# Contracting the value matmuls of the 16 by 16 corner over 128 rows instead of 32 in a forgetting-attention layer

## The chip, the cores and the metric

The kernel runs on one core of one Trainium2 chip. The metric is the device time of one execution in microseconds (us); lower is better. Engines are called as the profile calls them: PE is TensorE's matmuls, PEld its weight loads, DVE VectorE, ACT ScalarE, POOL GpSimd, SP the engine that issues DMAs.

## The reference

One layer over 16 learned tokens followed by 2048 tokens of width 1024. What matters here is its attention, 16 heads of width 64:

```
s = q_t . k_s * 64**-0.5 + c_t - c_s        (c: running sum of log sigmoid of a forget logit)
mask: key position <= query position
p = softmax(s);  o_t = sum_s p[t, s] v_s
```

The rest of the layer is an input norm, one input projection, a pooling mixer, gates, an output projection and an output norm. All of it is float32. The kernel gets float32 accuracy from pairs of float32r numbers (a high part and a low part, `ph` and `pl` of the exponentials).

## The kernel before, in words

The program has three stages. The first computes the projections, the row maxima of the attention and the pooling mixer. The second (phase B) does the attention, and mixes the matmuls of the output projection into it as filler (tiles `d<-wh,xm`, `d<-wl,xm`). The third finishes the output projection and the norm. Every engine but SP executes its instructions in the order in which the code emits them (`in_order`).

In phase B the work goes in 64 chunks: one for each head `h` and each block `j` of 512 queries, `j` from 0 to 3. The keys of a chunk are taken in units, written by `units(j)`: the 4j+1 full units of 128 keys by 512 queries, then a unit of 400 queries, then a last unit with three places of 272, 144 and 16 queries, since the causal mask leaves less and less of the block. The 16 learned tokens shift keys against queries, so that the last 16 queries of a block still need 16 keys of the next key tile. This is the 16 by 16 corner, the place with `w == NM`. Its keys stand in rows 112 to 127: the score matmuls take the 128 keys that end with these 16, and `mask_c` sends all rows but the last 16 to exp(-1e30) = 0. The corner's value rows are loaded into rows 112 to 127 of the tile `vc`.

For each unit `m` the loop emits `emit_s(m)` (scores into PSUM tile `s`, four buffers; two exponentials on ACT), up to four filler matmuls, `emit_pl(m)` (the low part `pl` on DVE, which frees the buffer of `s`), and `emit_pv(m - 4)`: the value matmuls, with the exponentials as the moving operand and the values as the weights. `xo` sums the products with `ph`; `yo` sums the products with `pl` and, through the weights `zo` (64 columns of zeros and two of ones), the softmax denominator. In chunks with j from 1 to 3 two more matmuls, `yo<-th,zo` and `yo<-tl,zo`, add a denominator that POOL and DVE have summed. At the end of a chunk ACT copies `yo` out (`c1`, shown as `c`), and DVE combines it with `xo`.

In the kernel before, the three value matmuls of a corner use rows 96 to 127 of weights and moving operand alone; only these rows of `vc` are set to zero (two memsets on POOL, one for each of the two sets of buffers).

Of the kernel before, what the change touches and what calls it, by code (L numbers as in the profile page):

```python
# [16 lines left out]
P = 128  # L17
NM = 16
# [5 lines left out]
DH = 64  # L24
# [11 lines left out]
def f32(ap):  # L36
    return ap.bitcast(F32)
# [3 lines left out]
def kernel(  # L41
# [20 lines left out]
    nc = tc.nc  # L62
# [35 lines left out]
    nc = NC()  # L98
    mm = nc.tensor.matmul

    def dma(out, in_):
        out, in_ = out[tuple(slice(None) for _ in out.shape)], in_[tuple(slice(None) for _ in in_.shape)]
        nc.sync.dma_start(
            out.bitcast(F32) if out.dtype == F32R else out, in_.bitcast(F32) if in_.dtype == F32R else in_
        )
# [12 lines left out]
    def dtile(name, shape, dt):  # L118
        return dram.tile(shape, dt, tag=name, name=name)

    # rows of a head: c high and low, k high, k low, q low, q high, -max high and low
    kqd = dtile("kqd", [H, 260, L], F32)
    vd = [dtile(f"vd{c}", [8, P, NKT, P], F32) for c in range(2)]
    fd = dtile("fd", [H, L], F32)
# [321 lines left out]
    off = fp.tile([P, 1], F32, tag="off", name="off")  # L446
# [279 lines left out]
    def kv_set(pl, s):  # L726
        ka = pl.tile([68, L], F32R, tag=f"ka{s}", name="ka")
        kb = pl.tile([P, L], F32R, tag=f"kb{s}", name="kb")
        vt = pl.tile([P, NKT - 1, P + 2], F32R, tag=f"vt{s}", name="vt")
        vc = pl.tile([P, 4, P + 2], F32R, tag=f"vc{s}", name="vc")  # L730
        nc.gpsimd.memset(f32(ka[0:2, :]), 1.0)
        nc.gpsimd.memset(f32(vc[96:P]), 0.0)
        for v in (vt, vc):
            nc.gpsimd.memset(f32(v[:, :, P : P + 2]), 1.0)
        kas.append(ka)
        kbs.append(kb)
        vts.append((vt, vc))

    kv_set(kvs[0], 0)
    zo = kvs[0].tile([P, DH + 2], F32R, tag="zo", name="zo")  # L740
    nc.vector.memset(f32(zo[:, 0:DH]), 0.0)
# [10 lines left out]
    def load_kv(h, i):  # L752
        ka, kb, (vt, vc) = kas[h % 2], kbs[h % 2], vts[h % 2]
        half, h8 = divmod(h, 8)
        if i == loaded[h]:
            loaded[h] += 1
            c0, c1 = 512 * i + (NM if i else 0), 512 * (i + 1) + NM
            dma(ka[2:68, c0:c1], kqd[h, 0:66, c0:c1])
            dma(kb[:, c0:c1], kqd[h, 2:130, c0:c1])
            dma(vt[:, 4 * i : 4 * i + 4, 0:P], vd[half][h8, :, 4 * i : 4 * i + 4, :])  # L760
            dma(vc[P - NM : P, i, 0:P], vd[half][h8, :NM, 4 * i + 4, :])
# [6 lines left out]
    def load_q(n):  # L768
        h, j = seqn[n]
        qa = qas[n % NQ]  # L770
        qb = kvs[0].tile([P, 512], F32R, tag="qb", name="qb", bufs=NQ)
        sl = slice(NM + 512 * j, NM + 512 * (j + 1))
        dma(qa[0:2, :], kqd[h, 258:260, sl])
        dma(qa[4:68, :], kqd[h, 194:258, sl])
        dma(qb, kqd[h, 130:258, sl])
        qt[n] = (qa, qb)
# [6 lines left out]
    fetched = [0]  # L783

    def prefetch(n, nv):
        """Loads at most one piece of keys and values ahead of head order, and queries two steps ahead."""
        k = 0
        while kvq:
            h, i = kvq[0]
            near = any(t[0] == h and t[1] >= i for t in seqn[n : n + 2])  # L790
            if h >= 2 and last_use[h - 2] >= nv or (k and not near) or first_use[h] > n + 5:
                break
            load_kv(h, i)
            kvq.popleft()
            k += 1
        while fetched[0] < min(NB, n + 3):
            load_q(fetched[0])
            fetched[0] += 1
# [12 lines left out]
    pso = pool(phase_b, "pso", space=PSUM)  # L811
    bp = pool(phase_b, "bp")
    kv_set(bp, 1)

    wsl = {}
# [60 lines left out]
    order = [t for t in (*range(4, 8), *range(4), *range(8, 12)) if t not in EARLY] + EARLY  # L876
# [36 lines left out]
    def after(d, fn):  # L913
        state["id"] = state.get("id", 0) + 1
        post.append((state["round"] + d, state["id"], fn))

    def chunk_end(p, j):
        sl = slice(512 * j, 512 * (j + 1))
        st = gt.tile([P, 8], F32, tag="st", name="st", bufs=2)
        dma(st, sd[p][:, sl].rearrange("a (b c) -> a b c", c=8))  # L920

        def s1():
            nc.vector.reciprocal(st, st)
            dma(rd[p][:, sl].rearrange("a (b c) -> a b c", c=8), st)
            rb = gt.tile([P, 512], F32, tag="rb", name="rb", bufs=2)
            for e in range(2):
                dma(rb[DH * e : DH * (e + 1), :], rd[p][e : e + 1, sl].broadcast_to([DH, 512]))
            sg = gt.tile([P, 512], F32, tag="sg", name="sg", bufs=2)
            dma(sg, gd[p][:, sl])

            def s2():
                a = araw.pop((p, j))
                for t in (rb, sg):
                    nc.gpsimd.tensor_tensor(out=a, in0=a, in1=t, op=ALU.mult)

                def s3():
                    am = gt.tile([P, 2, 512], F32R, tag="am", name="am", bufs=2)
                    nc.vector.tensor_copy(out=am[:, 0], in_=a)
                    nc.gpsimd.tensor_tensor(out=am[:, 1], in0=a, in1=f32(am[:, 0]), op=ALU.subtract)
                    dma(xmix[0][:, p, :, sl], am)  # L940
                    gated.add((p, j))

                after(2, s3)

            after(4, s2)

        after(4, s1)
# [67 lines left out]
    def emit_pv(m):  # L1015
        n, i, u, nu = seq[m]
        h, j = seqn[n]
        vt, vc = vts[h % 2]
        ph, pl, places = units_state.pop(m)
        if i == 0:  # L1020
            xy[0] = pso.tile([P, 512], F32, tag="x", name="xo", bufs=2)
            xy[1] = pso.tile([P, 512], F32, tag="y", name="yo", bufs=1)
        xo, yo = xy[0], xy[1]
        last_u = i == nu - 1
        np_ = len(places)
        full = i < 4 * j
        for idx, (kt, q0, w, off) in enumerate(places):
            first = i == 0 and idx == 0
            sl = slice(off, off + w)
            rows, v = (slice(96, P), vc[:, j]) if w == NM else (slice(0, P), vt[:, kt])  # L1030
            mm(
                xo[:, q0:512], v[rows, 0:P], ph[rows, sl],
                start=first, stop=last_u and idx == np_ - 1,
            )
            if not full:
                mm(yo[0 : DH + 2, q0:512], zo[rows], ph[rows, sl], start=first, stop=False)
        if last_u and j:
            for t in accs.pop(n):
                mm(yo[0 : DH + 2, :], zo, t, start=False, stop=False)
        for idx, (kt, q0, w, off) in enumerate(places):  # L1040
            rows, v = (slice(96, P), vc[:, j]) if w == NM else (slice(0, P), vt[:, kt])
            mm(
                yo[0 : DH + 2, q0:512], v[rows, DH:], pl[rows, off : off + w],
                start=full and i == 0 and idx == 0, stop=last_u and idx == np_ - 1,
            )
        if last_u:
            c1 = bp.tile([65, 512], F32, tag="c1", name="c1", bufs=2)
            nc.scalar.copy(out=c1, in_=yo[0:65, :])
            t = bp.tile([DH, 512], F32, tag="t", name="t", bufs=2)
            nc.vector.tensor_tensor(out=t, in0=xo[DH:P, :], in1=c1[0:DH, :], op=ALU.add)  # L1050
            p, e = divmod(h, 2)
            if e == 0:
                araw[p, j] = gt.tile([P, 512], F32, tag="araw", name="araw", bufs=6)
            sl = slice(512 * j, 512 * (j + 1))
            nc.vector.tensor_tensor(
                out=araw[p, j][DH * e : DH * (e + 1), :], in0=xo[0:DH, :], in1=t, op=ALU.add
            )
            dma(sd[p][e : e + 1, sl], c1[64:65, :])
            if e == 1:
                after(1, lambda: chunk_end(p, j))  # L1060
# [19 lines left out]
    def weight(m):  # L1080
        n, i, u, nu = seq[m] if m < nseq else seq[-1]
        return 2.0 if i < nu - 2 else 1.0

    LEAD, TAIL = 24, 24
    for m in range(nseq + LAG):
        if m < nseq:
            emit_s(m)
        if m >= LEAD:
            if m < nseq - TAIL:
                w = [weight(t) for t in range(m, nseq - TAIL)]  # L1090
# [3 lines left out]
            k = min(int(state["fill"]), 4)  # L1094
# [139 lines left out]
```

## Time and profile before

| what | value |
|---|---|
| median of 3 runs | 2431.03 us (2428.52 to 2432.9) |
| span of the profiled execution | 2432.5 us |
| PE busy | 2366.8 us, 97% of the span, 11706 matmuls |
| PEld busy | 1947.5 us, 80% |
| DVE busy | 1430.4 us, 59% |
| ACT busy | 960.6 us, 39% |
| POOL busy | 716.2 us, 29% |

The span runs from the first to the last instruction of one profiled execution. No separate device time of that execution is given; its span lies inside the range of the three timed runs, 1.5 us above their median. PE is busy almost all the time. Every row shows L86, the line of the helper that emits all instructions in order, so the rows are told apart by their tiles (`out<-in`) and shapes: `32*128 32x16` is a matmul over 32 rows with 128 columns of weights and 16 columns streamed. Matmuls overlap in the records (the next starts before the one before has ended), so what a matmul costs is read from the distance between the starts of two neighbours, not from its duration.

### The profile page before, as it was taken

To read this page: it belongs to the slowest core of one execution; us is meant where nothing else is said; L and a number is where in the kernel's file an instruction comes from. 1 tells how busy PE (TensorE), PEld (TensorE's weight loads), DVE (VectorE), ACT (ScalarE), POOL (GpSimd) and SP (SyncE) were. 2 spreads that over 40 slices of the span, in tenths; PEclk is the share of its full clock that TensorE was granted. 3 is DMA by queue.
4 is the path that set the end of the run, shared out by engine and by line. 5 is a ranking of instruction groups with operands and counts; after the bars stand their busy time and mean duration, and the time that the engine had idled before them with its cause. 6 is when DMAs were issued, how large, how long until landed. Compare 5 with 4: busy or idle time off the path is not lost.

```text
span 2432.5 us, 32725 instructions
## 1 busy us (share of the span) xinstructions
PE 2366.8 (97%) x11706; PEld 1947.5 (80%) x11706; DVE 1430.4 (59%) x2116; ACT 960.6 (39%) x1813; POOL 716.2 (29%) x531
## 2 busy tenths in 40 slices
PE   6999999999999999999999899999999999999998
PEld 5778799898898988988887677777777777776787
DVE  6631145644655556545433578778778777777356
ACT  4431221211212222111111577777777777766000
POOL 4730021222223314230101134344353544444000
PEclk9999999999999999999999999999999999999999
DMA  7853222222222212222223657566566657555955
GB/s 254 262 162 92 61 85 61 96 63 78 88 62 88 81 60 88 68 92 75 75 81 111 174 159 210 153 189 181 168 187 179 199 168 215 161 164 158 286 187 164
DMA packets 317506, 333.59 MB, mean 137 GB/s; under 512 B 27744, under 2 KB 241072, under 8 KB 317312
## 3 DMA queue, kind: packets, MB, share of 16 engines
q1 hardware_dynamic: 317344, 331.51, 44.4%
q8 instruction: 92, 1.51, 0.3%
q14 instruction: 70, 0.57, 0.1%
HBM read 207.43 MB, written 124.00 MB: 136 GB/s over the span
## 4 chain that ended last, share of the span: by engine, by line
PE 91%; DVE 3%; DMA 2%; issue 1%; ACT 1%; POOL 0%; SPq 0%; DVEq 0%; ACTq 0%; POOLq 0%
PE d L86 59%; PE s L86 12%; PE yo L86 8%; PE mx L86 6%; PE xo L86 5%; DVE pl L86 1%; PE tr L86 1%; DMA xm<-xa 1%; DMA wu<-in_wut_dram 0%; SPq L86 0%; DVE acc L86 0%; DMA xt<-in_x_dram 0%; DVE s L86 0%; DMA wv<-in_wv_dram 0%; DMA kb<-kqd 0%
## 5 line engine op out<-in xcount | busy, mean ns | idle before, releaser
L86 PE MATMUL d<-hh,wh 128*128 128x412 f32 (+2 forms) x1472 | 561.4, 381 | 0.0
L86 PE MATMUL d<-hl,wh 128*128 128x412 f32 (+2 forms) x1472 | 538.6, 366 | 0.0
L86 PE MATMUL d<-hh,wl 128*128 128x412 f32 (+2 forms) x1472 | 538.4, 366 | 0.0
L86 DVE TENSOR_REDUCE mxs<-mx 128x1 f32<-128x912 f32 (+14 forms) x416 | 358.3, 865 | 279.1 <-PE mx L86 274.5
L86 DVE TENSOR_TENSOR pl<-s,ph 128x512 fp32r<-128x512 f32 (+2 forms) x576 | 376.3, 664 | 185.8 <-ACT s L86 179.6
L86 ACT ACTIVATE ph<-s 128x512 fp32r<-128x512 f32 (+2 forms) x576 | 335.0, 582 | 186.6 <-PE s L86 171.9
L86 PE MATMUL d<-wh,xm 128*128 128x512 f32 x1024 | 355.0, 403 | 4.6 <-DMA xm<-xa 3.8
L86 ACT ACTIVATE s<-s 128x512 f32<-128x512 f32 (+2 forms) x576 | 332.4, 577 | 0.0
L86 PEld LDWEIGHTS d<-hl,wh 128*128 128x128 f32 x1472 | 278.5, 189 | 23.1
L86 PEld LDWEIGHTS d<-hh,wl 128*128 128x128 f32 x1472 | 277.1, 188 | 23.4
L86 PEld LDWEIGHTS d<-hh,wh 128*128 128x128 f32 x1472 | 280.7, 191 | 18.2
L86 PE MATMUL s<-qa,ka 68*128 68x512 f32 (+4 forms) x704 | 265.2, 377 | 15.9 <-DVE pl L86 15.9
L86 POOL TENSOR_TENSOR wl<-wst,wh 128x1024 fp32r<-128x1024 f32 x40 | 96.2, 2405 | 576.4 <-ACT wh L86 576.3
L86 PE MATMUL s<-qb,kb 128*128 128x512 f32 (+4 forms) x704 | 253.0, 360 | 0.0
L86 POOL TENSOR_TENSOR tu<-ph 128x512 f32<-128x512 f32 x144 | 190.9, 1328 | 154.4 <-ACT ph L86 128.3
L86 PE MATMUL xo<-ph,vt 128*128 128x512 f32 (+3 forms) x640 | 233.0, 368 | 0.0
L86 PEld LDWEIGHTS d<-wh,xm 128*128 128x128 f32 x1024 | 193.5, 190 | 44.4 <-issue 3.3
L86 PE MATMUL yo<-pl,vt 128*66 128x512 f32 (+3 forms) x640 | 223.7, 366 | 0.9 <-ACT c L86 0.9
L86 PE MATMUL mx<-ka,qa 66*128 66x512 f32 (+5 forms) x704 | 199.4, 350 | 6.6 <-ACT qa L86 3.8
L86 PE MATMUL d<-wl,xm 128*128 128x512 f32 x512 | 205.6, 402 | 0.0
L86 PEld LDWEIGHTS s<-qa,ka 68*128 68x128 f32 x704 | 134.8, 191 | 71.6 <-DVE pl L86 27.4
L86 PEld LDWEIGHTS mx<-ka,qa 66*128 66x128 f32 x704 | 133.0, 190 | 23.8 <-ACT qa L86 5.2
(143 smaller groups left out, 3079.0 us busy)
## 6 DMA issues: line engine op xcount, KB each, us to landing
xm<-xp SPq DMA_DIRECT2D x32, 1024.0 KB
xm<-xa SPq DMA_DIRECT2D x20, 1024.0 KB
vd<-vs SPq DMA_DIRECT2D x32, 512.0 KB
vt<-vd SPq DMA_DIRECT2D x64, 256.0 KB
qb<-kqd SPq DMA_DIRECT2D x64, 256.0 KB
xa<-am SPq DMA_DIRECT2D x32, 512.0 KB
xp<-pm SPq DMA_DIRECT2D x32, 412.0 KB
kqd<-lo SPq DMA_DIRECT2D x64, 206.0 KB
```

The source lines that it names most:

```text
L86: return in_order(f(*a, **k))
```

## The change

The three value matmuls of each corner take all 128 rows of `vc`, `zo`, `ph` and `pl` instead of rows 96 to 127, and the two memsets clear all of `vc`, so that rows 0 to 111 of it are zeros. The result is the same, since those rows multiply exponentials that are zero. No instruction is added, removed or moved on any engine: the order of the program's rows is the same on PE, DVE, ACT and SP, and on POOL two rows change their shape, from 32x520 to 128x520.

```diff
-        nc.gpsimd.memset(f32(vc[96:P]), 0.0)
+        nc.gpsimd.memset(f32(vc), 0.0)
...
-            rows, v = (slice(96, P), vc[:, j]) if w == NM else (slice(0, P), vt[:, kt])
+            v = vc[:, j] if w == NM else vt[:, kt]
             mm(
-                xo[:, q0:512], v[rows, 0:P], ph[rows, sl],
+                xo[:, q0:512], v[:, 0:P], ph[:, sl],
                 start=first, stop=last_u and idx == np_ - 1,
             )
             if not full:
-                mm(yo[0 : DH + 2, q0:512], zo[rows], ph[rows, sl], start=first, stop=False)
+                mm(yo[0 : DH + 2, q0:512], zo, ph[:, sl], start=first, stop=False)
...
-            rows, v = (slice(96, P), vc[:, j]) if w == NM else (slice(0, P), vt[:, kt])
+            v = vc[:, j] if w == NM else vt[:, kt]
             mm(
-                yo[0 : DH + 2, q0:512], v[rows, DH:], pl[rows, off : off + w],
+                yo[0 : DH + 2, q0:512], v[:, DH:], pl[:, off : off + w],
                 start=full and i == 0 and idx == 0, stop=last_u and idx == np_ - 1,
             )
```

## Rows read from the trace of the kernel before

**Rows 1.** The page, part 4: shares of the chain that ended last, by engine.

```profile
PE 91%; DVE 3%; DMA 2%; issue 1%; ACT 1%; POOL 0%; SPq 0%; DVEq 0%; ACTq 0%; POOLq 0%
```

**Rows 2.** Windows: phase B; us, busy us (instructions) of PE, PEld, DVE, ACT, POOL, clock, DMA.

```profile
1359.20:2246.30 887.10, 870.29 (x4347) 657.53 (x4345) 689.16 (x1061) 649.64 (x1242) 377.22 (x288) 0.99 0.61 180
```

**Rows 3.** Timeline of PE, end of one chunk with j = 1: start us, duration us, instruction.

```profile
1809.31 0.29 PE L86 MATMUL yo<-ph,zo 128*66 128x272 f32 x1
1809.44 0.23 PE L86 MATMUL xo<-ph,vt 128*128 128x144 f32 x1
1809.50 0.23 PE L86 MATMUL yo<-ph,zo 128*66 128x144 f32 x1
1809.66 0.27 PE L86 MATMUL xo<-ph,vc 32*128 32x16 f32 x1
1809.80 0.20 PE L86 MATMUL yo<-ph,zo 32*66 32x16 f32 x1
1809.92 0.45 PE L86 MATMUL yo<-th,zo 128*66 128x512 f32 x1
1810.21 0.39 PE L86 MATMUL yo<-tl,zo 128*66 128x512 f32 x1
1810.44 0.35 PE L86 MATMUL yo<-pl,vt 128*66 128x272 f32 x2
1810.72 0.22 PE L86 MATMUL yo<-pl,vc 32*66 32x16 f32 x1
1810.87 0.50 PE L86 MATMUL s<-qa,ka 68*128 68x512 f32 x1
1811.21 0.39 PE L86 MATMUL s<-qb,kb 128*128 128x512 f32 x1
```

**Rows 4.** Timeline of PEld at the same place.

```profile
1809.44 0.14 PEld L86 LDWEIGHTS yo<-ph,zo 128*66 128x66 f32 x1
1809.66 0.18 PEld L86 LDWEIGHTS xo<-ph,vc 32*128 32x128 f32 x1
...
1809.92 0.13 PEld L86 LDWEIGHTS yo<-th,zo 128*66 128x66 f32 x1
1809.98 0.14 PEld L86 LDWEIGHTS yo<-tl,zo 128*66 128x66 f32 x1
...
1810.72 0.13 PEld L86 LDWEIGHTS yo<-pl,vc 32*66 32x66 f32 x1
1810.87 0.19 PEld L86 LDWEIGHTS s<-qa,ka 68*128 68x128 f32 x1
1810.98 0.19 PEld L86 LDWEIGHTS s<-qb,kb 128*128 128x128 f32 x1
```

**Rows 5.** Timeline of PE, end of one chunk with j = 0, first and last.

```profile
1800.01 0.23 PE L86 MATMUL yo<-ph,zo 128*66 128x144 f32 x1
...
1801.26 0.40 PE L86 MATMUL s<-qb,kb 128*128 128x512 f32 x1
```

**Rows 6.** Groups of PE by shape: busy us, mean ns, idle us before.

```profile
L86 PE MATMUL xo<-ph,vc 32*128 32x16 f32 x64 | 17.4, 272 | 0.0
```

**Rows 7.** Timeline of PE, the scores of one corner.

```profile
1804.11 0.26 PE L86 MATMUL s<-qa,ka 68*128 68x16 f32 x1
1804.22 0.26 PE L86 MATMUL s<-qb,kb 128*128 128x16 f32 x1
```

**Rows 8.** Waits of PEld in phase B: us in total, times, longest us.

```profile
PEld s L86 <- DVE pl L86: 27.4, 27, 3.0
PEld yo L86 <- ACT c L86: 2.7, 6, 1.2
```

**Rows 9.** Waits of PEld from 1355 to 1400 us.

```profile
PEld s L86 <- DVE pl L86: 8.9, 8, 2.4
```

**Rows 10.** Windows from 1355 to 1400 us, instructions on tile `vc` alone (PE, PEld, POOL).

```profile
1355.00:1400.00 45.00, 1.48 (x6) 0.93 (x6) 0.64 (x2) 0.96 0.77 216
```

**Rows 11.** Timeline of POOL, the second of the two memsets.

```profile
1359.24 0.53 POOL L86 MEMSET vc<- 32x520 f32 x1 [27.39 <-PE d L86]
```

## The prediction

> **What bounds the kernel now.** I read the page first, for who sets the end: in the chain of work that ended last PE holds 91% [rows 1]. Then the windows, for the stage of the change: phase B takes 887.1 us, PE is busy in 870.3 of them, DVE in 689.2 (78%) and ACT in 649.6 (73%) [rows 2]. So a microsecond that PE does not need there is, to first order, a microsecond of the kernel, and the question is only what PE spends at the corners.
>
> For that I read the timeline of PE around one corner, start to start [rows 3]. Full-height matmuls are spaced by their columns: 272 columns take 0.13 us (1809.31 to 1809.44), 144 columns 0.06 (1809.44 to 1809.50), 512 columns 0.23 (1810.21 to 1810.44). The neighbours of the 32-row matmuls are not. After the 144 columns at 1809.50 the corner's `xo` matmul starts 0.16 later, the corner's `yo` 0.14 after it, `th` 0.12 after that, though 16 columns are streamed in each of the last two; `th` itself, 512 columns, holds its successor up for 0.29 instead of 0.23; the corner's `pl` matmul starts 0.28 after the pair of 272 and 144 columns, which need 0.13 + 0.06; then 0.15 and 0.34 follow.
>
> The weight loads say why [rows 4]. A load normally runs ahead of its matmul: that of the 144-column `yo` starts at 1809.44, while the matmul before it starts, 0.06 ahead of its own. At the four places where the number of rows changes (128 to 32, 32 to 128, and both again) the load starts together with its own matmul: 1809.66, 1809.92, 1810.72, 1810.87, the same starts as in [rows 3]. So at each change of height the load is not started early, and PE stands bare for it. Loads of one height follow each other quicker: 66 columns in 0.06 (1809.92 to 1809.98), 128 columns in 0.11 (1810.87 to 1810.98).
>
> **The change part by part.** It removes no instruction. It makes three matmuls and three loads per chunk 128 rows high, 64 chunks [rows 6], and with that removes all four changes of height.
>
> The kernel before has no 128-row matmul of 16 columns with these weights, so I build the new spacing from the nearest rows: each step is the longer of the columns streamed ahead and the next load.
> - 144-column `yo` to corner `xo`: the load of 128 columns, 0.11 (before: 0.16).
> - corner `xo` to corner `yo`: the load of 66 columns, 0.06 (before: 0.14).
> - corner `yo` to `th`: 0.06 (0.12); `th` to `tl`: 0.23 (0.29); `tl` to `pl`: 0.23 (0.23).
> - the `pl` pair: 0.13 + 0.06 = 0.19 (0.28).
> - corner `pl` to `s<-qa`: the load of 128 columns, 0.11 (0.15); `qa` to `qb`: 0.23 (0.34).
>
> The new sum is 0.11 + 0.06 + 0.06 + 0.23 + 0.23 + 0.19 + 0.11 + 0.23 = 1.22 us. Before, it is 1811.21 - 1809.50 = 1.71 us [rows 3]: 0.49 us less. A chunk with j = 0 lacks `th` and `tl`: 1801.26 - 1800.01 = 1.25 us before [rows 5], and 0.11 + 0.06 + 0.06 + 0.19 + 0.11 + 0.23 = 0.76 after, again 0.49 less. Over 64 chunks that is 31.4 us.
>
> The uncertain step is 0.06 for a 66-column load behind 16 columns. The other bound is the nearest 16-column neighbours of full height: the two score matmuls of a corner start 0.11 apart [rows 7], but load 128 columns of weights each. If all 16-column steps cost 0.11, the three steps at 0.06 (into corner `yo`, into `th`, into corner `pl`) rise by 0.05 each, and a chunk gains 0.34, in all 21.8 us. Below that lies no gain at all (the second rival). I take 0.06, because [rows 4] shows it on this very load (`zo`, 66 columns), and because [rows 3] has a 66-column matmul 0.06 behind 144 columns, so such a load fits into 0.06.
>
> The memset grows from 32 to 128 rows with the same 520 elements in each. It takes 0.53 us [rows 11]; I bound it between 0.53 (rows in parallel) and 2.1 (four times). POOL stood idle for 27.39 us before it, and only the loads into the second set wait for it, so it costs nothing; if that cover were gone, 1.6 us, twice.
>
> What is late next: PE reaches the next scores 0.49 us sooner after each corner, and a buffer of `s` is free only when DVE has made `pl`. Before, PEld waits for this 27 times [rows 8], in 576 units. Where it waits, a saving made just ahead turns into waiting. If each of the 27 swallowed one whole saving, 27 x 0.49 = 13.2 us would be given back. They come in bunches, though: in the first 45 us there are 8 of them [rows 9] and only 3 chunk ends (6 matmuls on `vc`, two of an end [rows 10]), so 8 waits can swallow 3 savings. By that ratio 27 waits swallow about 10 savings, 4.9 us. The other wait that can grow is that for ACT's copy of `yo`, whose only buffer the next chunk needs: 6 times, 2.7 us in all [rows 8]. The copy starts when the last `yo` ends, and so moves ahead with it; I take nothing for it. After the change DVE would be busy for 689 of about 861 us, 80%, still no bound.
>
> The sum against the profiled execution: 2432.5 - 31.4 + 4.9 = 2406.0. Its span is 1.5 us above the median of the runs; against the median that is 2404.5, and I say 2404 us, 1.1% less.
>
> **The rivals.**
>
> *The small step costs 0.11 whatever the weights.* Then 21.8 us are gained, less a third of the given-back time, since the savings are smaller by a third (3.3 us): 2431.0 - 18.5 = 2412.5. For it speaks [rows 7], the only full-height matmuls of 16 columns; against it the 0.06 between two loads [rows 4].
>
> *The change does not do what it says: the gaps belong to the narrow corner, not to its height.* The loads of 32 rows last no less than those of 128 (0.18 against 0.19 [rows 4]), so no load gets cheaper or dearer, and the three matmuls keep their place. Then the time stays at 2431. Against it speak the 0.29 of `th` and the 0.34 of `s<-qa`: they are full-height, have 512 columns, and are held up only because the matmul ahead is of another height. The Trainium skill ("TensorE: Matmul & The Clock Gate", "Why this matters for your kernels") says that one matmul over 32 rows takes the same time as one over 128, the gain lying in several at once; by that rule alone the sum would be zero and the time 2431. The same skill ("TensorEngine Tiling (Array Packing)", "Key Properties") says that a change of tiling mode drains the engine; by that rule the height costs something after all, and the late loads of [rows 4] agree with it.
>
> *Slower: a full-height load cannot start while a full-height matmul is in flight.* Then each of five loads would wait for the end of the matmul ahead: 0.23 + 0.18 into corner `xo`, 0.27 + 0.14 into corner `yo`, 0.20 + 0.14 into `th`, 0.23 + 0.14 into corner `pl` (taking the 144-column `pl` as long as the 144-column `yo`), 0.22 + 0.19 into `s<-qa`, in sum 1.94 [rows 3, 4]; with `th`, `tl` and `qa` at 0.23 each and the 0.13 of the first `pl`, 2.76 us against 1.71. That is +1.05 us for 64 chunks, +67 us, 2498. It decides from two of the five on: a serial step costs some 0.3 more than in my list (0.41 against 0.11 into corner `xo`), so two use up the gain of 0.49. Against it: the score matmuls of a corner are full-height, last 0.26 each and still start 0.11 apart [rows 7]; serial they would be 0.45 apart. The Trainium skill ("TensorE: Matmul & The Clock Gate", Part 3, "The mechanism") has such a rule: loads overlap matmuls in flight only where the row group differs; by it the time would be the 2498 above, and the 0.11 of [rows 7] does not agree.
>
> **How the numbers follow.** My forecast gets 0.76, the dearer small step 0.11, no effect 0.08, slower 0.03; 0.02 are left for a gain beyond the forecast's. The forecast's own range goes from 2431.0 - 31.4 = 2399.6 (nothing given back) to 2431.0 - 31.4 + 13.2 = 2412.8 (every wait swallows a saving). The first rival lies inside it or at its edge; with the spread of the runs (2 us either way) the range is 2397 to 2415. It leaves out the other two rivals. About 0.2% (4.9 us) is what a measurement of this kernel can tell from no change: faster 0.88, same 0.08, slower 0.04.
>
> **What the profile after would show.** The loads of corner `xo`, `th`, corner `pl` and the next scores start ahead of their matmuls again; corner `xo` starts 0.11 us behind the 144 columns, corner `yo` and `th` 0.06 apart; `th` to `tl` takes 0.23; the whole end of a chunk 1.2 us instead of 1.7. Phase B is about 27 us shorter, and the wait of the score loads for DVE grows by some 5 us. If the small steps stand at 0.11, the first rival is right; if 1.7 us remain, the second. I would be wrong most easily if DVE's waits multiplied, so that PE's gain came out as idle time: then PE's ends would be shorter and phase B not.

## The result and the profile after

| | before | after |
|---|---|---|
| median | 2430.08 us (4 runs, 2428.52 to 2432.9) | 2403.17 us (4 runs, 2401.99 to 2404.49) |
| span of the profiled execution | 2432.5 us | 2402.8 us |
| ratio of the times, 95% interval | | 0.9881 [0.9867, 0.9895] |

The kernel became 26.9 us faster; 2404 had been forecast. In a second comparison beside other kernels (label e8_changed_again below) the same change gave 2402.76 against 2430.31 us.

The chain of work that ended last, page part 4, answers to [rows 1]; PE's share has not moved, it is still the bound:

```profile
PE 91%; DVE 3%; DMA 2%; ACT 1%; issue 1%; POOL 0%; SPq 0%; DVEq 0%; ACTq 0%; POOLq 0%
```

The window of phase B, with the columns of [rows 2] and over the same instructions (4347 matmuls, 4345 loads in both): 857.4 us, where it was 887.1, and PE busy 840.2 instead of 870.3. The 30 us lie in the stage of the change and in PE's own work. The mean granted clock of TensorE is 0.992 of its full 2.4 GHz in either profiled execution, so the clock does not explain the difference.

```profile
1360.05:2217.47 857.42, 840.23 (x4347) 644.45 (x4345) 686.58 (x1061) 648.67 (x1242) 380.80 (x288) 0.99 0.63 186
```

The timeline of PE at the end of the same chunk as in [rows 3]:

```profile
1791.93 0.29 PE L86 MATMUL yo<-ph,zo 128*66 128x272 f32 x1
1792.06 0.23 PE L86 MATMUL xo<-ph,vt 128*128 128x144 f32 x1
1792.13 0.23 PE L86 MATMUL yo<-ph,zo 128*66 128x144 f32 x1
1792.19 0.22 PE L86 MATMUL xo<-ph,vc 128*128 128x16 f32 x1
1792.27 0.20 PE L86 MATMUL yo<-ph,zo 128*66 128x16 f32 x1
1792.33 0.43 PE L86 MATMUL yo<-th,zo 128*66 128x512 f32 x1
1792.60 0.39 PE L86 MATMUL yo<-tl,zo 128*66 128x512 f32 x1
1792.83 0.35 PE L86 MATMUL yo<-pl,vt 128*66 128x272 f32 x2
1793.01 0.17 PE L86 MATMUL yo<-pl,vc 128*66 128x16 f32 x1
1793.04 0.48 PE L86 MATMUL s<-qa,ka 68*128 68x512 f32 x1
1793.35 0.40 PE L86 MATMUL s<-qb,kb 128*128 128x512 f32 x1
```

The same eleven rows, in the same order. From the 144-column `yo` to the second score matmul it was 1.71 us; now it is 1793.35 - 1792.13 = 1.22. The weight loads there (PEld, as [rows 4]):

```profile
1792.13 0.19 PEld L86 LDWEIGHTS xo<-ph,vc 128*128 128x128 f32 x1
1792.24 0.14 PEld L86 LDWEIGHTS yo<-ph,zo 128*66 128x66 f32 x1
1792.30 0.14 PEld L86 LDWEIGHTS yo<-th,zo 128*66 128x66 f32 x1
...
1792.95 0.14 PEld L86 LDWEIGHTS yo<-pl,vc 128*66 128x66 f32 x1
1793.02 0.19 PEld L86 LDWEIGHTS s<-qa,ka 68*128 68x128 f32 x1
1793.12 0.19 PEld L86 LDWEIGHTS s<-qb,kb 128*128 128x128 f32 x1
```

The loads run ahead again. That of the corner's `xo` starts at 1792.13, with the matmul before it and 0.06 ahead of its own; before, it started together with its own matmul. The loads now follow each other at their own pace, 0.10 to 0.11 us after a load of 128 columns, 0.06 to 0.07 after one of 66. The load for `s<-qa` starts only 0.02 ahead of its matmul, but it follows the load before it at that pace.

The waits of PEld in phase B, as [rows 8], and the memset, as [rows 11]:

```profile
PEld s L86 <- DVE pl L86: 26.3, 26, 3.6
PEld yo L86 <- ACT c L86: 4.3, 7, 1.6
```

```profile
1360.09 0.53 POOL L86 MEMSET vc<- 128x520 f32 x1 [27.41 <-PE d L86]
```

DVE's wait has not grown, that for ACT's copy has by 1.6 us. Clearing 128 rows takes the 0.53 us of 32.

### The profile page after: what moved, and what is told of

Its sections match the earlier page's. It is cut to its first block, busy times and chain, and to the rows that moved or that the text cites. A ratio compares the mean times of both kernels' runs of the same rounds, so it can differ in the third digit from the quotient of the medians.

```text
span 2402.8 us, 32724 instructions
## 1 busy us (share of the span) xinstructions
PE 2336.9 (97%) x11706; PEld 1934.7 (81%) x11706; DVE 1427.3 (59%) x2116; ACT 959.5 (40%) x1813; POOL 719.3 (30%) x531
## 4 chain that ended last, share of the span: by engine, by line
PE 91%; DVE 3%; DMA 2%; ACT 1%; issue 1%; POOL 0%; SPq 0%; DVEq 0%; ACTq 0%; POOLq 0%
PE d L86 60%; PE s L86 12%; PE yo L86 8%; PE mx L86 6%; PE xo L86 5%; DMA xm<-xa 1%; PE tr L86 1%; DVE pl L86 1%; ACT ph L86 0%; DMA wu<-in_wut_dram 0%; DMA xt<-in_x_dram 0%; DVE s L86 0%; DMA wv<-in_wv_dram 0%; ACT s L86 0%; DVE mxs L86 0%
## 5 line engine op out<-in xcount | busy, mean ns | idle before, releaser
L86 POOL TENSOR_TENSOR wl<-wst,wh 128x1024 fp32r<-128x1024 f32 x40 | 96.2, 2404 | 576.7 <-ACT wh L86 576.6
L86 PEld LDWEIGHTS s<-qa,ka 68*128 68x128 f32 x704 | 134.9, 192 | 69.0 <-DVE pl L86 26.3
```

The costliest lines, as they stand in the source:

```text
L86: return in_order(f(*a, **k))
```

## The experiments

Two accounts were to be told apart. The height account: each *change* of the number of rows costs PE a fixed time, whichever matmuls stand there. The matmul account: each of the three 32-row matmuls is dear in itself. After the change both are gone, so its result fits either. In each experiment below I read the same stretch of PE's timeline, from the start of the 272-column `yo` to the start of the second score matmul of the same chunk: 1811.21 - 1809.31 = 1.90 us before [rows 3], 1793.35 - 1791.93 = 1.42 after. The chunk shown is a usual one: the median of this stretch over the chunks with j from 1 to 3 is 1.90 us before and 1.42 after. All times are medians; each of the two sets of four kernels shared its runs of the kernel before (2429.06 us for the first four, 2430.31 for the others).

**One of the three matmuls back on 32 rows.** In the changed kernel:

```diff
+            rows = slice(96, P) if w == NM else slice(0, P)
...
-                yo[0 : DH + 2, q0:512], v[:, DH:], pl[:, off : off + w],
+                yo[0 : DH + 2, q0:512], v[rows, DH:], pl[rows, off : off + w],
```

> The changed kernel, with the corner's pl matmul alone back on rows 96 to 127: two changes of height per chunk, one 32-row matmul. Height theory (each change of the number of rows costs a fixed price, and the four of a chunk cost 0.48 us together): in the kernel before, the steps around this matmul took 0.159 + 0.150 + 0.338 us against 0.067 + 0.028 + 0.314 after the change, 0.24 us more, so 64 x 0.24 = 15 us of the 27 come back and the time is about 2418 us. Matmul theory (each of the three 32-row matmuls is dear in itself, a third of the gain each): 9 us come back, 2412 us.

Measured 2417.17 us, ratio to before 0.9946 [0.9934, 0.9958]; the gain over the kernel before of its own set is 11.9 us, where the whole change gains 26.9 to 27.6, so some 15 us came back. The matmul account had 9. PE's timeline:

```profile
1798.18 0.29 PE L86 MATMUL yo<-ph,zo 128*66 128x272 f32 x1
...
1799.07 0.35 PE L86 MATMUL yo<-pl,vt 128*66 128x272 f32 x2
1799.35 0.22 PE L86 MATMUL yo<-pl,vc 32*66 32x16 f32 x1
1799.50 0.50 PE L86 MATMUL s<-qa,ka 68*128 68x512 f32 x1
1799.84 0.40 PE L86 MATMUL s<-qb,kb 128*128 128x512 f32 x1
```

The stretch takes 1.66 us, 0.24 more than with none. Around the one 32-row matmul the steps are again 0.28, 0.15 and 0.34, as in [rows 3].

**One of the three on 128 rows.** In the kernel before, with all of `vc` cleared:

```diff
-                xo[:, q0:512], v[rows, 0:P], ph[rows, sl],
+                xo[:, q0:512], v[:, 0:P], ph[:, sl],
```

> The kernel before, with the corner's xo matmul alone on 128 rows: still four changes of height per chunk (before the corner's yo, before th or the pl pair, and on both sides of the corner's pl), two 32-row matmuls instead of three. Height theory: nothing is gained but what the order of a load changes, 2427 to 2431 us. Matmul theory: a third of the gain, 9 us, 2421 us.

Measured 2426.62 us, ratio 0.9989 [0.998, 0.9997]: a gain of 2.4 us, far from 9.

```profile
1800.40 0.29 PE L86 MATMUL yo<-ph,zo 128*66 128x272 f32 x1
...
1800.67 0.22 PE L86 MATMUL xo<-ph,vc 128*128 128x16 f32 x1
1800.81 0.22 PE L86 MATMUL yo<-ph,zo 32*66 32x16 f32 x1
...
1802.26 0.40 PE L86 MATMUL s<-qb,kb 128*128 128x512 f32 x1
```

The change of height has only moved from the corner's `xo` to the corner's `yo`, and the stretch takes 1.86 us (1.84 as the median of the chunks with j from 1 to 3). The 0.04 to 0.06 that is saved fits the load that stands bare: 66 columns now (0.06), 128 before (0.11).

**The three 32-row matmuls together.** In the kernel before, the order of the last unit is written out (x, y, l: the matmuls into `xo`, with `zo`, with `pl`; 0, 1, 2: the places of 272, 144 and 16 queries):

```diff
-        x0 y0 x1 y1 x2 y2 th tl l0 l1 l2
+        x0 y0 x1 y1 x2 y2 l2 th tl l0 l1
```

> The kernel before with its three 32-row matmuls in one row (the corner's pl matmul moved up behind the corner's yo, ahead of th and tl): the same three 32-row matmuls, two changes of height per chunk instead of four. Height theory: half of the gain, 12 to 15 us, 2415 to 2418 us. Matmul theory: no gain, 2430 us.

Measured 2416.2 us, ratio 0.9945 [0.9933, 0.9957]: 12.9 us faster with the same three 32-row matmuls. This alone is not to be had with the matmul account.

```profile
1800.40 0.29 PE L86 MATMUL yo<-ph,zo 128*66 128x272 f32 x1
...
1800.75 0.27 PE L86 MATMUL xo<-ph,vc 32*128 32x16 f32 x1
1800.89 0.20 PE L86 MATMUL yo<-ph,zo 32*66 32x16 f32 x1
1800.95 0.20 PE L86 MATMUL yo<-pl,vc 32*66 32x16 f32 x1
1801.08 0.45 PE L86 MATMUL yo<-th,zo 128*66 128x512 f32 x1
...
1802.06 0.39 PE L86 MATMUL s<-qb,kb 128*128 128x512 f32 x1
```

The stretch takes 1.66 us. Between 32-row neighbours the corner's `pl` stands 0.06 behind the corner's `yo`, the step of a 66-column load: a 32-row matmul after a 32-row matmul is as cheap as a full one after a full one.

**The three apart.** The same kernel, the other way:

```diff
-        x0 y0 x1 y1 x2 y2 th tl l0 l1 l2
+        x0 y0 x2 x1 y2 y1 th tl l0 l2 l1
```

> The kernel before with its three 32-row matmuls apart (the corner's xo ahead of the 144-column xo, the corner's yo ahead of the 144-column yo, the corner's pl between the two others): the same matmuls, six changes of height per chunk instead of four. Height theory: two more changes at about 0.12 us each, 64 x 0.24 = 15 us more, 2445 us. Matmul theory: no difference, 2430 us.

Measured 2445.9 us, ratio 1.0076 [1.0062, 1.009]: 16.8 us slower.

```profile
1813.84 0.29 PE L86 MATMUL yo<-ph,zo 128*66 128x272 f32 x1
1814.05 0.27 PE L86 MATMUL xo<-ph,vc 32*128 32x16 f32 x1
...
1814.52 0.43 PE L86 MATMUL yo<-ph,zo 32*66 32x16 f32 x2
...
1815.46 0.22 PE L86 MATMUL yo<-pl,vc 32*66 32x16 f32 x1
1815.61 0.28 PE L86 MATMUL yo<-pl,vt 128*66 128x144 f32 x1
...
1816.01 0.39 PE L86 MATMUL s<-qb,kb 128*128 128x512 f32 x1
```

The stretch takes 2.17 us. (The row with x2 holds the corner's `yo` and the 144-column `yo`.) So over changes of height per chunk the stretch takes:

| changes | kernel | stretch us | median us |
|---|---|---|---|
| 0 | after | 1.42 | 2402.8 |
| 2 | one back on 32 rows | 1.66 | 2417.2 |
| 2 | three together | 1.66 | 2416.2 |
| 4 | before | 1.90 | 2429.1, 2430.3 |
| 6 | three apart | 2.17 | 2445.9 |

0.12 to 0.135 us for each change; over 64 chunks, by the medians, some 7 to 8.5 us of the whole for one change per chunk. The new orders by themselves do not explain it: by the prediction's rule (a step is the longer of the columns streamed and the next load), both orders would take 1.41 us at full height, as the order of the changed kernel does. No run has these two orders at full height.

**64 rows instead of 32.** In the kernel before:

```diff
-        nc.gpsimd.memset(f32(vc[96:P]), 0.0)
+        nc.gpsimd.memset(f32(vc[64:P]), 0.0)
...
-            rows, v = (slice(96, P), vc[:, j]) if w == NM else (slice(0, P), vt[:, kt])
+            rows, v = (slice(64, P), vc[:, j]) if w == NM else (slice(0, P), vt[:, kt])
```

(the second in both loops).

> The kernel before with the corner's three value matmuls on rows 64 to 127 (vc cleared there): 64-row matmuls in place of 32-row ones at the same four changes. Height theory (any change of the number of rows costs): as before, 2430 us, within some 4 us. If only 32-row matmuls cost: 2403 us.

Measured 2429.99 us, ratio 0.9997 [0.9985, 1.0009]: no difference.

```profile
1805.06 0.29 PE L86 MATMUL yo<-ph,zo 128*66 128x272 f32 x1
...
1805.41 0.27 PE L86 MATMUL xo<-ph,vc 64*128 64x16 f32 x1
...
1806.96 0.40 PE L86 MATMUL s<-qb,kb 128*128 128x512 f32 x1
```

The stretch takes 1.90 us again. 64 rows are as much another height as 32 are. 68 rows are not: `s<-qa,ka` contracts over 68, and its step to the 128-row `s<-qb,kb` for 16 columns is 0.11 in [rows 7], the time of a 128-column load.

In these kernels the first row moves with the height (32 rows begin at row 96, 64 at row 64, 68 at row 0), and no run separates the two. The trace of before has one place that does, ahead of phase B: the transposes of the 16 learned tokens, which take rows 0 to 15 (two rows of PE, one of PEld).

```profile
52.40 0.28 PE L86 MATMUL d<-ph,ul 128*128 128x256 f32 x1
52.61 0.66 PE L86 MATMUL tr<-ident,xt 16*128 16x16 f32 x8
52.61 0.57 PEld L86 LDWEIGHTS tr<-ident,xt 16*128 16x128 f32 x8
```

The 256 columns hold the first transpose up for 0.21 us, though matmuls of the same shape ahead of it start 0.12 apart (52.28 to 52.40), and its load starts together with it. Transposes of 128 rows show no such gap: one follows 512 columns by 0.23 (78.69 to 78.92). So the late load comes with few rows that begin at row 0 too. It is a single place of the program, and no price per change is taken from it.

**The corner left out.** The changed kernel without the three value matmuls of a corner (their part of the output is left out):

```diff
+        places = [t for t in places if t[2] != NM]
```

> The changed kernel without the three value matmuls of a corner (their part of the output is left out): what a full-height corner still costs. If the steps are set by the longer of streamed columns and next weight load, 0.16 us go ahead of th and 0.06 ahead of the next scores, 64 x 0.22 = 14 us: 2389 us. If 16 columns cost almost nothing: 2400 us or more.

Measured 2390.91 us, ratio to before 0.9839 [0.9826, 0.9852]: 11.9 us below the changed kernel, where 14 had been expected and 3 or less by the other account.

```profile
1784.52 0.29 PE L86 MATMUL yo<-ph,zo 128*66 128x272 f32 x1
...
1785.71 0.39 PE L86 MATMUL s<-qb,kb 128*128 128x512 f32 x1
```

The stretch takes 1.19 us, 0.23 less than in the changed kernel: 0.11 + 0.06 + 0.06, what the loads of the three take. In this order of the rest, making them shorter still can give no more than these 12 us.

**Another order.** If a step is the longer of the columns streamed and the next load, a wide matmul should stand ahead of a 128-column load. The changed kernel with

```diff
-        x0 y0 x1 y1 x2 y2 th tl l0 l1 l2
+        x2 y0 x0 x1 y1 y2 th tl l2 l1 l0
```

> The changed kernel with the nine value matmuls of a chunk's last unit in another order, so that wide matmuls stand ahead of the 128-column loads (corner xo, 272-column yo, 272-column xo, 144-column xo, 144-column yo, corner yo; and the pl matmuls as corner, 144, 272). If a step is the longer of streamed columns and next load, with 0.11 us for a 128-column load and 0.055 for 66 columns, the first six take 0.49 us instead of 0.53 and the pl three 0.25 instead of 0.30: 64 x 0.1 = 6 us, 2397 us. If loads do not bound these steps: 2403 us.

Measured 2396.29 us, ratio to before 0.9861 [0.9848, 0.9875]; the changed kernel beside it had 2402.76, so this order gains 6.5 us more, and is the fastest here that computes everything.

```profile
1787.14 0.17 PE L86 MATMUL xo<-ph,vc 128*128 128x16 f32 x1
...
1788.13 0.39 PE L86 MATMUL yo<-pl,vt 128*66 128x144 f32 x2
1788.35 0.40 PE L86 MATMUL s<-qa,ka 68*128 68x512 f32 x1
1788.59 0.40 PE L86 MATMUL s<-qb,kb 128*128 128x512 f32 x1
```

From the `pl` pair (144, then 272 columns) the score matmuls follow at 0.22 and 0.24, where the changed kernel had 0.31 for the last step: the 128-column load now hides behind the 272 columns. From the first value matmul to the second score matmul it is 1788.59 - 1787.14 = 1.45 us. In the changed kernel the first is

```profile
1791.81 0.29 PE L86 MATMUL xo<-ph,vt 128*128 128x272 f32 x1
```

so that it took 1793.35 - 1791.81 = 1.54. The 0.09 less is what had been expected (0.04 in the first six, 0.05 in the `pl` matmuls).

**The changed kernel beside these.**

> The changed kernel itself beside the others on the same chip: 2403 us; the gain over the kernel before 26 to 30 us.

Measured 2402.76 us, ratio 0.9887 [0.9874, 0.9901]: 27.6 us gained.

## Why the prediction was right, point by point

**PE bounds phase B, so its microseconds are the kernel's.** Right: PE's busy time in phase B fell by 30.1 us, the phase by 29.7.

**The gap belongs to the change of height.** Right, and shown: the time follows the number of changes (0, 2, 4, 6), with the same matmuls in three of the five rows of the table. That the number of rows decides, and not the first of them, rests on the one place at 52.61. The late loads of [rows 4] were the right place to read it. Of the two rules of the Trainium skill that had been weighed in the second rival, the drain at a change of tiling mode ("TensorEngine Tiling (Array Packing)", "Key Properties") agrees with the 0.12 us per change.

**1.22 us per chunk end.** Right as a sum: 1.22 measured. The single steps were placed differently. I had the corner's `xo` 0.11 behind the 144 columns and the scores 0.11 behind the corner's `pl`; the rows show 0.06 and 0.03, and the time turns up later, corner `xo` to corner `yo` 0.08 instead of 0.06, `th` to `tl` 0.27 instead of 0.23 and `qa` to `qb` 0.31 instead of 0.23. The loads have about the predicted spacing (0.11 after 128 columns, 0.06 after 66), and the matmul of a load can be recorded as started while the load still runs: `s<-qa` starts at 1793.04, its load lasts from 1793.02 to 1793.21. So single steps are not to be read as prices, sums up to the next wide matmul are. One argument of the prediction falls with that: against the second rival it took the 0.29 after `th` and the 0.34 after `s<-qa` as signs of the height, but 0.27 and 0.31 of them remain without any change of height. The second rival is refuted by the time and by the experiments instead. The first rival, 0.11 for every small step, fell: the sum would have been 1.37.

**4.9 us given back to waits for DVE.** This term was wrong: these waits went from 27 (27.4 us) to 26 (26.3 us), so nothing went there. My step was that a wait swallows a saving made ahead of it. In the sum over phase B it did not. The score matmul ahead of one and the same chunk end waits for DVE in both kernels, first before, then after (the idle time ahead of it stands in brackets):

```profile
1469.57 0.50 PE L86 MATMUL s<-qa,ka 68*128 68x512 f32 x1 [0.66 <-DVE pl L86]
```

```profile
1464.57 0.50 PE L86 MATMUL s<-qa,ka 68*128 68x512 f32 x1 [0.67 <-DVE pl L86]
```

PE comes there 5 us earlier, and the wait is as long as it was. The `pl` of DVE that it waits for had also come earlier, by the same 5.00 us, before and after:

```profile
1468.91 2.19 DVE L86 TENSOR_TENSOR pl<-s,ph 128x432 fp32r<-128x432 f32 x4
```

```profile
1463.91 2.19 DVE L86 TENSOR_TENSOR pl<-s,ph 128x432 fp32r<-128x432 f32 x4
```

So here DVE had moved ahead with PE. This is read from one chunk end; no run tests it for the others. The wait I had put at nothing, for ACT's copy of `yo`, grew by 1.6 us.

**The sum.** The ends of the chunks lost 64 x 0.49 = 31.4 us, phase B and the profiled spans 29.7, the medians 26.9 and 27.6. Of the 1.7 us between the first two, 1.6 can be the copy's wait. The 2.8 between 29.7 and 26.9 say only which executions were profiled: that of after took 2404.49 us, 1.7 more than its span and 1.3 above the median; if the 1.7 held before too, that of before took some 2434.2 (an estimate), 4.1 above its median. The forecast of 2404 owes part of its closeness to luck: without the 4.9 us, whose stated cause was not there, the sum was 2399.6, 3.6 below the measured 2403.17. That difference is itself hardly clear of the noise (the interval of the ratio is 3.4 us wide to either side).

**No effect; slower.** Both rivals fell with the result. That a full-height load cannot start beside a full-height matmul is refuted by the load at 1792.13, under way while the 144 columns stream.

**The memset** took 0.53 us for 128 rows: the lower bound.

## What to carry to other kernels

In this kernel a matmul that contracts over few rows was not cheaper than a full one, and between full ones it cost two changes of height (0.24 us). Where you find that, pad it with zeros to the height of its neighbours (26.9 us here), or put all such matmuls side by side (12.9 us). Read the start of the weight load against the start of its own matmul and against the load before it: where a load starts together with its matmul and later than the pace of the loads, PE stands bare. With narrow matmuls, count the loads as well as the columns, and put a wide one ahead of each 128-column load (6.5 us).

## What the runs showed of the hardware that was not expected

- 64 rows cost as much as 32 at the same four changes (2429.99 against 2430.31 us), though the step from 68 to 128 rows costs no more than its load (0.11 us).
- What a change costs seems to depend on the load behind it: with the first change ahead of 66 instead of 128 columns the stretch took 1.86 instead of 1.90 us, about the difference of the two loads.
- Within the lower height, a step can be as short as within the full one: with the three together, the corner's `pl` starts 0.06 us behind the corner's `yo`.
